# A delta rule with both heads stacked on partitions: 64 columns in place of 128

## The chip, the core and the metric

The kernel runs on one core of a Trainium2 chip. The metric is device time in microseconds (us), the median of several executions. The engines are named as the profile names them: PE is TensorE's matmul, PEld its weight load, DVE is VectorE, ACT is ScalarE, POOL is GpSimd, and SP issues the transfers (DMAs).

## The reference

One inference step of a hybrid layer. 256 prompt tokens and 64 sample tokens (8 sequences of 8) go through RMSNorm and one wide projection. Branch A is an RWKV-7 recurrence with 16 heads of width 64, branch B a gated linear recurrence with 8 heads of 128. Both are projected, gated, merged, projected once more and normalised. The change lies in branch A, whose recurrence per token is

```python
sa = einsum('nhvk,nhk->nhv', s, kk_t)
s = (s * w_t[:, :, None, :] - sa[..., None] * (kk_t * a_t)[:, :, None, :]
     + v_t[..., None] * k_t[:, :, None, :])
y_t = einsum('nhvk,nhk->nhv', s, r_t)
```

A token's state `s` has been changed by every token before it (the delta rule). For a chunk of 64 tokens this is a triangular system: with a strictly triangular matrix `N` of products between keys, the right-hand sides are solved by the inverse of `1 - N`, and the solutions update the state.

## The kernel before

All arithmetic is fp32. Large products are made of three fp32r matmuls (high by high, high by low, low by high): each weight block `raw` of 128 x 1024 is cast by ACT to `whi`, DVE subtracts to `wlo`, and PE multiplies 128 x 128 pieces with `hhi` or `hlo` of 320 token columns, into the PSUM tile `mps`. Call one such matmul a **big** one. Small matmuls of branches A and B are plain fp32; the built program has one matmul for each, and the profile shows two passes of it on PE, each with its own weight load. A transpose is one pass.

The program has three stages. First a start (norm, constants). Then a recorded stage: for each of 8 pairs of heads, eight projection tiles of 48 big matmuls, the function `rwkv` for the pair (two heads of branch A) and `hgrn` (one head of branch B), then seven gate tiles. Last come the projections of the branches (L492 to L494) and the output projection (L1678 to L1684), which the change does not touch.

In the recorded stage nothing is issued when it is written. `V`, `S`, `G`, `T` and `Y` (DVE, ACT, POOL, PE, SP) are proxies that record; `Recorder.order` then deals all operations out by a list schedule: every operation has a cost and a latency from a formula of its shape, dependences are found from the tiles' partitions and columns (in PSUM from partitions alone), big matmuls keep their order, and small matmuls go between them as soon as their operands should be there. So a change of a few shapes moves nearly every row. Every instruction of this stage has the line L199 in the profile (the recorder's call); one goes by its tiles' names. Six PSUM banks are lent to the small products; the profile calls each of them `bank`. The framework that emits the operations in that order adds the semaphore waits itself, and it does so by tile: a matmul that writes a bank waits for a copy that was emitted before it and reads that bank, also where the two touch different partitions.

PE's array can be cut into tiles of rows by columns. Each matmul carries its cut: 128x128 for big and most small ones, 128x32 for `side_by_side` groups of 32-column products, 64x128 and 64x64 for two others. A profile row shows it as the weights' partitions by columns, `128*32`.

Inside `rwkv`, a pair's 256 prompt tokens are four chunks of 64 (`ci`, two outer by two inner), and the names are:

- `g2`: masked products of keys and queries; `nd`: the part to be inverted; `yz`: the inverses of the four chunks, on 128 partitions; `ys`: the samples' inverse; `M`, `pp`, `xt`: pieces with which `yz` is finished.
- `pr`, `psr`: PSUM tiles with the products that the right-hand sides start from, head 0 on partitions 0 to 63, head 1 on 64 to 127. They are the first 28 matmuls of a group of 70, all in 128x32 cuts, whose other 42 are branch B's. `rhs`, `rhs2`: right-hand sides; `uv`: solutions and values; `st`: the state after a chunk, `sf` the same decayed; `bk`, `arp`: keys, and decayed keys and queries.
- `chunks()`: for each chunk, PE multiplies `arp` with `st` (chunks 1 to 3), DVE adds into `rhs`, PE multiplies `yz` with `rhs`, ACT copies into `uv`, PE multiplies `bk` with `uv`, DVE makes `st`, ACT makes `sf`. At the end the state is transposed (`pso`), copied to `so` and stored. `samples()` does it once with `ys`.

Before, the inverse `yz` of one chunk has 64 token rows of one position in the pair of chunks, for both heads side by side in the columns; `rhs` therefore has the two heads side by side too, 128 columns wide, and `st` is a 128 x 128 tile of which the two diagonal blocks are the heads' states:

```python
pu = aps("pu")
T.matmul(pu[:, :128], yz[:, c_, cp]..., rt..., start=True, stop=True)
...
sn = at("st", (128, 128), bufs=4)
V.scalar_tensor_tensor(sn, pd[:, :128], fc, sf, op0=ALU.mult, op1=ALU.add)
```

Of the kernel before, what the change touches and what calls it, by code (L numbers as in the profile page):

```python
# [13 lines left out]
ALU = mybir.AluOpType  # L14
# [5 lines left out]
NT = NP_ + NS  # L20
# [407 lines left out]
def hybrid_step(ctx, tc, x_prompt, x_sample, state_rwkv, state_hgrn, state_shift, norm_g, w_in,  # L428
# [80 lines left out]
    with tc.tile_pool(name="start", bufs=1) as st, \  # L509
# [78 lines left out]
        G.tensor_copy(seqm[HS[1]], seqm[low_])  # L588
        own8 = ctile([128, 8], "own8")
# [242 lines left out]
    def ring(pool, tag, shape, bufs, dt, size, clear=False):  # L832
# [17 lines left out]
        if len(shape) == 2:  # L850
# [5 lines left out]
             "w1": 384, "w2": 320, "w3": 320, "ks": 128, "ye": 192, "ket": 256, "o": NT}  # L856
# [55 lines left out]
    def rwkv(p, r, k, v, za):  # L912
# [129 lines left out]
        for c_ in range(2):  # L1042
            S.copy(nd[HS[c_]], g2[HS[c_], c_:4:2, 0])
# [55 lines left out]
        V.tensor_mul(ys[0:64].rearrange("p h (b j) -> p h b j", j=8), yes[:, :, None, :].to_broadcast([64, 2, 8, 8]),  # L1099
                     seqm[0:64, None, :, None].to_broadcast([64, 2, 8, 8]))  # L1100
        yt = at("yt", (128, 4, 32), tag="uK")
        V.transpose(yt.rearrange("p x (j g) -> p x g j", g=8), ye)
        for q_ in (1, 3, 0, 2):
            (S.copy if q_ % 2 else G.tensor_copy)(yz[quads[q_], q_ // 2, :, :, halves[q_ % 2]],
                                                  yt[quads[q_]].rearrange("p (a h) t -> p a h t", h=2))
# [3 lines left out]
        for cp in range(2):  # L1109
            T.matmul(ps[:, 128 * cp:128 * cp + 128], M[:, cp].rearrange("p h t -> p (h t)"), yz[:, :, cp, :, 32:64], start=True, stop=True)  # L1110
# [7 lines left out]
        for c_ in range(2):  # L1118
            own = quads[2 * c_]
            S.copy(yz[own, c_, :, :, 32:64], ps[own, :256].rearrange("p (a c h t) -> p a c h t", a=2, c=2, h=2)[:, :, c_])  # L1120
# [31 lines left out]
        def chunks():  # L1152
            st_ = None
            for ci in range(4):
                cp, c_ = ci // 2, ci % 2
                tk = HS[c_]
                rt = at("rhs", (128, 2, 64))
                if st_ is None:
                    S.copy(rt[tk, 0], pr[HS[0], 0:64])
                    S.copy(rt[tk, 1], pr[HS[1], 0:64])  # L1160
                    rv = at("rv", (128, 3, 64), tag="ye")
                    S.copy(rv.rearrange("p c v -> p (c v)"), pr[:, 64:256])
                else:
# [12 lines left out]
                sn = at("st", (128, 128), bufs=4)  # L1176
                fc = f[:, 4 + ci:5 + ci]
                if st_ is None:
                    V.tensor_scalar(sn, pd[:, :128], fc, 0.0, op0=ALU.mult, op1=ALU.add)
                else:  # L1180
                    V.scalar_tensor_tensor(sn, pd[:, :128], fc, sf, op0=ALU.mult, op1=ALU.add)
# [15 lines left out]
        def samples():  # L1197
            rhs = at("rhs2", (128, 2, 64))
            S.copy(rhs[0:64, 0], psr[HS[0], :64])
            S.copy(rhs[0:64, 1], psr[HS[1], :64])  # L1200
            yield
            pu = aps("pu2")
            T.matmul(pu[:, :128], ys.rearrange("p h t -> p (h t)"), rhs.rearrange("p h t -> p (h t)"), start=True, stop=True)
            S.copy(uv[0:64, 4, 0], pu[HS[0], 0:64])
# [602 lines left out]
```

## Time and profile before

| | us |
|---|---|
| median of 3 runs | 1070.43 |
| lowest, highest | 1070.11, 1072.08 |
| the profiled execution's own time | 1070.57 |
| its span, first to last instruction | 1068.6 |
| recorded stage, about | 27 to 652 of the span |
| projections of the branches | about 652 to 910 |
| output projection and end | about 910 to the end |

The granted clock was 0.998 of full speed over the span. In rows of groups, the number after the bar is the busy time in us, then the mean of one in ns, then the idle time of the engine before them and what ended it. In rows of the timeline come start, length in us, engine, line, operation, tiles, the weights' cut, shape and count. PE's matmuls are pipelined: a big one is shown 0.31 us long, while the next starts 0.147 us after it, so what one costs is read from starts.

### The profile page before, as it was taken

The page shows a single profiled execution, that of the slowest core. Times are in us where ns is not written, and L with a number is a line of the kernel's source. Part 1 is how long each engine was busy: PE and PEld are TensorE (multiplying, and loading weights), DVE is VectorE, ACT ScalarE, POOL GpSimd, SP SyncE. Part 2 cuts the span into 40 slices and gives each one's busy share as a digit, 9 for nine tenths or more (in the row PEclk, how much of TensorE's full clock was granted, in tenths as well). Part 3 has the DMA queues.
Part 4 walks back from the last instruction along what each step waited for, and adds up shares of the span by engine and source line. Part 5 has one row for each costly group of instructions (what it writes and reads, how often), then busy time and mean ns, then how long its engine had stood idle before and what let it go on. Part 6 is the DMA issues. An engine that isn't in the chain of part 4 may idle for free.

```text
span 1068.6 us, 22991 instructions
## 1 busy us (share of the span) xinstructions
PE 1047.8 (98%) x8740; PEld 1011.1 (95%) x8740; DVE 758.5 (71%) x1608; ACT 696.9 (65%) x1616; POOL 124.1 (12%) x358
## 2 busy tenths in 40 slices
PE   7999999999999999999999999999999999999996
PEld 6999999999999999999999999999999999988886
DVE  8779889988988999989898856544443444446632
ACT  7757888878868878689688698444444444444412
POOL 9511201101111212011112000000000000000000
PEclk9999999999999999999999999999999999999999
DMA  6776585684774864866856837555455554587402
GB/s 203 195 178 180 131 210 139 157 225 122 185 195 120 210 188 119 203 162 158 210 131 178 214 110 206 168 158 164 142 154 150 147 157 143 155 295 245 169 20 98
DMA packets 356369, 178.77 MB, mean 167 GB/s; under 512 B 82013, under 2 KB 345440, under 8 KB 355684
## 3 DMA queue, kind: packets, MB, share of 16 engines
q1 hardware_dynamic: 355892, 176.01, 60.4%
q8 instruction: 68, 1.11, 0.4%
q10 hardware_dynamic: 368, 1.31, 0.3%
q14 instruction: 41, 0.34, 0.1%
HBM read 159.97 MB, written 17.32 MB: 166 GB/s over the span
## 4 chain that ended last, share of the span: by engine, by line
PE 87%; ACT 4%; DVE 4%; DMA 4%; issue 1%; SPq 0%; DVEq 0%; ACTq 0%
PE mps L199 39%; PE bank L199 10%; PE mps L494 5%; PE mps L493 5%; PE mps L492 5%; PE po L1678 3%; PE po L1679 3%; PE po L1680 3%; PE ppa L493 2%; PE ppb L494 2%; PE ppa L494 2%; PE ppb L493 2%; PE ppb L492 2%; PE ppa L492 2%; PE po L1684 1%; PE po L1683 1%
## 5 line engine op out<-in xcount | busy, mean ns | idle before, releaser
L199 PE MATMUL mps<-hhi,whi 128*128 128x320 f32 x1136 | 356.3, 314 | 0.0
L199 PE MATMUL mps<-hhi,wlo 128*128 128x320 f32 x1136 | 355.3, 313 | 0.4 <-DVE wlo L199 0.4
L199 PE MATMUL mps<-hlo,whi 128*128 128x320 f32 x1136 | 355.5, 313 | 0.0
L199 PEld LDWEIGHTS mps<-hhi,wlo 128*128 128x128 f32 x1136 | 213.6, 188 | 2.6 <-issue 1.5
L199 PEld LDWEIGHTS mps<-hlo,whi 128*128 128x128 f32 x1136 | 213.6, 188 | 2.4 <-issue 1.2
L199 PEld LDWEIGHTS mps<-hhi,whi 128*128 128x128 f32 x1136 | 213.7, 188 | 0.9 <-issue 0.4
L199 DVE TENSOR_TENSOR wlo<-raw,whi 128x1024 fp32r<-128x1024 f32 x140 | 171.5, 1225 | 24.9 <-ACT whi L199 23.6
L482 ACT CAST whi<-raw 128x1024 fp32r<-128x1024 f32 x82 | 85.7, 1048 | 146.5 <-PE mps L493 90.4
L483 DVE TENSOR_TENSOR wlo<-raw,whi 128x1024 fp32r<-128x1024 f32 x82 | 100.3, 1225 | 111.6 <-ACT whi L482 111.5
L199 ACT CAST whi<-raw 128x1024 fp32r<-128x1024 f32 x140 | 145.9, 1043 | 47.3 <-DMA raw<-in_w_in_dram 22.4
L494 PE MATMUL mps<-hhi,wlo 128*128 128x320 f32 x400 | 123.7, 309 | 0.1
L493 PE MATMUL mps<-hlo,whi 128*128 128x320 f32 x400 | 123.6, 309 | 0.0
L492 PE MATMUL mps<-hhi,whi 128*128 128x320 f32 x400 | 123.6, 309 | 0.0
L494 PEld LDWEIGHTS mps<-hhi,wlo 128*128 128x128 f32 x400 | 75.1, 188 | 0.3 <-DVE wlo L483 0.3
L492 PEld LDWEIGHTS mps<-hhi,whi 128*128 128x128 f32 x400 | 75.1, 188 | 0.0
L493 PEld LDWEIGHTS mps<-hlo,whi 128*128 128x128 f32 x400 | 75.1, 188 | 0.0
L1667 DVE TENSOR_TENSOR wlo<-raw,whi 128x1024 fp32r<-128x1024 f32 x32 | 38.5, 1222 | 37.5 <-ACT whi L1666 33.0
L1666 ACT CAST whi<-raw 128x1024 fp32r<-128x1024 f32 x32 | 33.0, 1051 | 47.7 <-DMA raw<-in_w_out_dram 19.5
L1678 PE MATMUL po<-whi,mhi 128*128 128x512 f32 x128 | 50.0, 391 | 0.0
L1679 PE MATMUL po<-whi,mlo 128*128 128x512 f32 x128 | 50.0, 391 | 0.0
L1680 PE MATMUL po<-wlo,mhi 128*128 128x512 f32 x128 | 50.0, 391 | 0.0
L492 PE MATMUL ppa<-yah,whi 128*128 128x320 f32 x128 | 39.7, 310 | 1.0 <-ACT yah L1613 1.0
(413 smaller groups left out, 1986.8 us busy)
## 6 DMA issues: line engine op xcount, KB each, us to landing
raw<-in_w_in_dram SPq DMA_DIRECT2D x194, 512.0 KB
raw<-in_w_out_dram SPq DMA_DIRECT2D x32, 512.0 KB
raw<-in_proj_a_dram SPq DMA_DIRECT2D x16, 512.0 KB
raw<-in_proj_b_dram SPq DMA_DIRECT2D x16, 512.0 KB
s<-in_state_hgrn_dram SPq DMA_DIRECT2D x8, 512.0 KB
ww<-scr SPq DMA_DIRECT2D x8, 512.0 KB
out_dram<-s SPq DMA_DIRECT2D x8, 512.0 KB
scrt<-ww SPq DMA_DIRECT2D x32, 120.0 KB
```

The costliest lines, as they stand in the source:

```text
L199: o.fn(*(real(x) for x in o.args), **{k: real(x) for k, x in o.kw.items()})
L482: S.copy(hi[:, ks], raw[:, ks])
L483: sub.tensor_sub(lo[:, ks], raw[:, ks], hi[:, ks].bitcast(F32))
L492: T.matmul(dst, hi[:, q, :], xhi[:, k, :], start=(k == 0), stop=False)
L493: T.matmul(dst, hi[:, q, :], xlo[:, k, :], start=False, stop=False)
L494: T.matmul(dst, lo[:, q, :], xhi[:, k, :], start=False, stop=(k == nk - 1))
L1666: S.copy(hi, raw)
L1667: V.tensor_sub(lo, raw, hi.bitcast(F32))
L1678: T.matmul(pt, h, hi, start=first, stop=False)
L1679: T.matmul(pt, l, hi, start=False, stop=False)
L1680: T.matmul(pt, h, lo, start=False, stop=end)
L1683: T.matmul(pt, h, hi, start=first, stop=False)
```

## The change

In the inverse, head and chunk change places: `yz` is now indexed by pair of chunks, chunk and head, and its 128 partitions hold head by token. The heads are stacked on partitions, block diagonal in the inverse, and everything that was two heads wide becomes 64 columns: `rhs` and `rhs2` (128 x 64), the results of `pr` and `pu` in `chunks()` and `samples()`, the state `st` and `sf`. Right-hand sides are copied or added by one instruction on 128 partitions, not two on 64. The state is made by two DVE instructions of 64 x 64. `nd` is copied by four ACT instructions, not two. The last state's transpose has 64 columns of weights and writes 64 partitions, and one copy takes it out. `ys` is filled on 128 partitions with a mask `seqh` that POOL makes at the start. As many matmuls and transfers are recorded as before.

```diff
+        seqh = ctile([128, 16], "seqh")
+        G.memset(seqh, 0.0)
+        for h in range(2):
+            G.tensor_copy(seqh[HS[h], 8 * h:8 * h + 8], seqm[HS[h]])
...
         for c_ in range(2):
-            S.copy(nd[HS[c_]], g2[HS[c_], c_:4:2, 0])
+            for h in range(2):
+                S.copy(nd[HS[h], :, c_], g2[HS[c_], c_:4:2, 0, h])
...
-        yes = at("yes", (64, 2, 8), tag="dns")
-        Y.dma_start(yes, sample_[1].rearrange("(h p) j -> p h j", h=2))
+        yes = at("yes", (128, 8), tag="dns")
+        Y.dma_start(yes, sample_[1])
...
             for ci in range(4):
-                rt = at("rhs", (128, 2, 64))
+                rt = at("rhs", (128, 64))
                 if st_ is None:
-                    S.copy(rt[tk, 0], pr[HS[0], 0:64])
-                    S.copy(rt[tk, 1], pr[HS[1], 0:64])
+                    S.copy(rt, pr[:, 0:64])
...
-                    T.matmul(ps[:, :128], arp[:, ci, 0].rearrange("p h t -> p (h t)"), st_, start=True, stop=True)
-                    for h in range(2):
-                        V.tensor_add(rt[tk, h], ps[HS[h], 64 * h:64 * h + 64], rv[HS[h], ci - 1])
+                    T.matmul(ps[:, :64], arp[:, ci, 0].rearrange("p h t -> p (h t)"), st_, start=True, stop=True)
+                    V.tensor_add(rt, ps[:, :64], rv[:, ci - 1])
                 yield
                 pu = aps("pu")
-                T.matmul(pu[:, :128], yz[:, c_, cp].rearrange("p h t -> p (h t)"), rt.rearrange("p h t -> p (h t)"), start=True, stop=True)
-                S.copy(uv[tk, ci, 0], pu[HS[0], 0:64])
-                S.copy(uv[tk, ci, 1], pu[HS[1], 64:128])
+                T.matmul(pu[:, :64], yz[:, cp, c_].rearrange("p h t -> p (h t)"), rt, start=True, stop=True)
+                for h in range(2):
+                    S.copy(uv[tk, ci, h], pu[HS[h], 0:64])
...
-                sn = at("st", (128, 128), bufs=4)
...
+                sn = at("st", (128, 64), bufs=4)
+                for h in range(2):
+                    own, new, fc = sn[HS[h]], pd[HS[h], 64 * h:64 * h + 64], f[HS[h], 4 + ci:5 + ci]
...
-                    sf = at("sf", (128, 128))
+                    sf = at("sf", (128, 64))
...
-            T.transpose(ps[:, :128], st_, ident)
+            T.transpose(ps[0:64, :128], st_, ident)
             so = at("so", (64, 2, 64))
-            for h in range(2):
-                S.copy(so[:, h], ps[HS[h], 64 * h:64 * h + 64])
+            S.copy(so.rearrange("p h k -> p (h k)"), ps[0:64, :128])
...
         def samples():
-            rhs = at("rhs2", (128, 2, 64))
-            S.copy(rhs[0:64, 0], psr[HS[0], :64])
-            S.copy(rhs[0:64, 1], psr[HS[1], :64])
+            rhs = at("rhs2", (128, 64))
+            S.copy(rhs, psr[:, :64])
```

Three places in the dealt order. In its rows, a result's shape is partitions by columns, and `waits` names the engines whose semaphores the instruction waits for.

**PE, the group of 70 of the first pair**, from its first row to the first of branch B (`s0t,az` and the first `uv,g` rows make `psr`, the other `uv,g` rows make `pr`). Before:

```order
L199 MATMUL bank_468<-s0t_516,az_519 32x64 x8
L199 MATMUL bank_468<-uv_514,g_0_521 32x64 x4
L199 MATMUL bank_467<-uv_514,g_0_521 32x64 x4
L199 MATMUL bank_467<-uv_514,g_0_521 32x64 [waits DMAHW3_49]
L199 MATMUL bank_467<-uv_514,g_0_521 32x64 x10
L199 MATMUL bank_467<-uv_514,g_0_521 32x64 [waits Activation_49]
L199 MATMUL bank_464<-s_0_528,qz 32x128 x8
```

And in the changed kernel:

```order
L199 MATMUL bank_471<-s0t_520,az_523 32x64 x8
L199 MATMUL bank_471<-uv_518,g_0_525 32x64 [waits DMAHW2_49]
L199 MATMUL bank_471<-uv_518,g_0_525 32x64 x3
L199 MATMUL bank_470<-uv_518,g_0_525 32x64 x4
L199 MATMUL bank_470<-uv_518,g_0_525 32x64 [waits DMAHW3_49]
L199 MATMUL bank_470<-uv_518,g_0_525 32x64 x11
L199 MATMUL bank_472<-s_0_532,qz 32x128 x8
```

The wait of the last `uv,g` matmul for an ACT copy is gone. Such a wait stood four times in the order before, in the groups of pairs 1, 4 (twice) and 8; in the changed order no group of 70 has one behind a copy into `rhs` or `rhs2`.

**ACT, the copies out of `psr` and `pr`** of the same pair. Before:

```order
L199 ACTIVATE dl_557<-F_533 128x1 [waits DVE_49]
L199 COPY rhs_0_544<-bank_468 64x64 [waits PE_49]
L199 COPY rhs_543<-bank_467 64x64 [waits PE_49] x2
L199 COPY ye_524<-bank_467 128x192
L199 COPY rhs_0_544<-bank_468 64x64
L199 ACTIVATE w_0_535<-R_534 128x128 [waits PE_49]
```

And in the changed kernel:

```order
L199 COPY pad_493<-mps 128x8x8 [waits Activation_49]
L199 COPY rhs_0_548<-bank_471 128x64 [waits PE_49]
L199 COPY rhs_547<-bank_470 128x64 [waits PE_49]
L199 COPY ye_528<-bank_470 128x192
L199 ACTIVATE w_0_539<-R_538 128x128 [waits DVE_49,PE_49]
```

Two copies on 128 partitions stand where four on 64 stood; each now reads both heads.

**PE, the transpose of the last state** (`ident,st`), second pair. Before:

```order
L199 MATMUL bank_467<-rl_558,jr_all 128x320 [waits DVE_49]
L199 MATMUL bank_463<-ident,s_0_505 128x128 [waits DMAHW1_49]
L199 MATMUL bank_463<-ident,s_0_505 128x128 x3
L199 MATMUL bank_464<-ident,st_550 128x128 [waits DVE_49]
L199 MATMUL mps<-hlo,whi 128x320
L199 MATMUL mps<-hhi,wlo 128x320
```

And in the changed kernel:

```order
L199 MATMUL mps<-hhi,wlo 128x320
L199 MATMUL mps<-hhi,whi 128x320
L199 MATMUL bank_470<-ident,st_554 64x128 [waits DVE_49]
L199 MATMUL mps<-hlo,whi 128x320
L199 MATMUL mps<-hhi,wlo 128x320
```

It writes 64 partitions where it wrote 128, and its cut in the built program is 128x64, with 128x128 matmuls on both sides; all eight pairs have it so. The other cuts change as often as before.

More of the change, by code (lines that the diff above doesn't have):

```diff
@@ L1094, in rwkv @@
                             prompt_[1].rearrange("(a h c b r) m -> a h b r c m", a=2, h=2, c=2, b=2)[a_, h, 0])
-        yes = at("yes", (64, 2, 8), tag="dns")
-        Y.dma_start(yes, sample_[1].rearrange("(h p) j -> p h j", h=2))
+        yes = at("yes", (128, 8), tag="dns")
+        Y.dma_start(yes, sample_[1])
         ys = at("ys", (128, 2, 64))
-        V.tensor_mul(ys[0:64].rearrange("p h (b j) -> p h b j", j=8), yes[:, :, None, :].to_broadcast([64, 2, 8, 8]),
-                     seqm[0:64, None, :, None].to_broadcast([64, 2, 8, 8]))
+        V.tensor_mul(ys.rearrange("p h (b j) -> p (h b) j", j=8), yes[:, None, :].to_broadcast([128, 16, 8]),
+                     seqh[:, :, None].to_broadcast([128, 16, 8]))
         yt = at("yt", (128, 4, 32), tag="uK")
@@ L1103, in rwkv @@
         for q_ in (1, 3, 0, 2):
-            (S.copy if q_ % 2 else G.tensor_copy)(yz[quads[q_], q_ // 2, :, :, halves[q_ % 2]],
-                                                  yt[quads[q_]].rearrange("p (a h) t -> p a h t", h=2))
+            (S.copy if q_ % 2 else G.tensor_copy)(yz[quads[q_], :, :, q_ // 2, halves[q_ % 2]],
+                                                  yt[quads[q_]].rearrange("p (a c) t -> p a c t", c=2))
         ps = aps("pP")
         for cp in range(2):
-            T.matmul(ps[:, 128 * cp:128 * cp + 128], M[:, cp].rearrange("p h t -> p (h t)"), yz[:, :, cp, :, 32:64], start=True, stop=True)
+            T.matmul(ps[:, 128 * cp:128 * cp + 128], M[:, cp].rearrange("p c t -> p (c t)"),
+                     yz[:, cp].rearrange("p c h t -> p h c t")[:, :, :, 32:64], start=True, stop=True)
         pp = at("pp", (128, 4, 64))
@@ L1119, in rwkv @@
             own = quads[2 * c_]
-            S.copy(yz[own, c_, :, :, 32:64], ps[own, :256].rearrange("p (a c h t) -> p a c h t", a=2, c=2, h=2)[:, :, c_])
+            S.copy(yz[own, :, :, c_, 32:64], ps[own, :256].rearrange("p (a h c t) -> p a h c t", a=2, c=2, h=2)[:, :, c_])
         bp = parts(bon)
@@ L1175, in chunks @@
                 T.matmul(pd[:, :128], bk[:, ci], uv[:, ci].rearrange("p h v -> p (h v)"), start=True, stop=True)
-                sn = at("st", (128, 128), bufs=4)
[L1177 to L1181, printed above, removed]
+                sn = at("st", (128, 64), bufs=4)
+                for h in range(2):
+                    own, new, fc = sn[HS[h]], pd[HS[h], 64 * h:64 * h + 64], f[HS[h], 4 + ci:5 + ci]
+                    if st_ is None:
+                        V.tensor_scalar(own, new, fc, 0.0, op0=ALU.mult, op1=ALU.add)
+                    else:
+                        V.scalar_tensor_tensor(own, new, fc, sf[HS[h]], op0=ALU.mult, op1=ALU.add)
                 st_ = sn
@@ L1197, in samples @@
         def samples():
-            rhs = at("rhs2", (128, 2, 64))
-            S.copy(rhs[0:64, 0], psr[HS[0], :64])
-            S.copy(rhs[0:64, 1], psr[HS[1], :64])
+            rhs = at("rhs2", (128, 64))
+            S.copy(rhs, psr[:, :64])
             yield
             pu = aps("pu2")
-            T.matmul(pu[:, :128], ys.rearrange("p h t -> p (h t)"), rhs.rearrange("p h t -> p (h t)"), start=True, stop=True)
-            S.copy(uv[0:64, 4, 0], pu[HS[0], 0:64])
-            S.copy(uv[0:64, 4, 1], pu[HS[1], 64:128])
+            T.matmul(pu[:, :64], ys.rearrange("p h t -> p (h t)"), rhs, start=True, stop=True)
+            for h in range(2):
+                S.copy(uv[0:64, 4, h], pu[HS[h], 0:64])
             fh = at("fh", (128, 8), dt=F32R)
@@ L1253, in rwkv @@
                 for h, o_, w in parts4:
-                    work.append(((py[o_:o_ + 32, cols_], states[ci - 1][:, o_:o_ + 32], arp[:, ci, 1, h]),
+                    work.append(((py[o_:o_ + 32, cols_], states[ci - 1][:, 32 * w:32 * w + 32], arp[:, ci, 1, h]),
                                  dict(start=True, stop=False)))
```

2 lines of the change are left out of this document (1 added, 1 removed).

## Prediction

> **What bounds the kernel now.** I read the page's first part first, then the busy times by stage, then PE's waits. The page:
>
> ```profile
> span 1068.6 us, 22991 instructions
> PE 1047.8 (98%) x8740; PEld 1011.1 (95%) x8740; DVE 758.5 (71%) x1608; ACT 696.9 (65%) x1616; POOL 124.1 (12%) x358
> ```
>
> The busy times of the stretch that holds the recorded stage (time, busy time of PE, PEld, DVE, ACT, POOL, clock, DMA share):
>
> ```profile
> 27.00:652.00 625.00, 620.33 (x6097) 606.40 (x6096) 539.83 (x1311) 499.13 (x1313) 99.64 (x305) 1.00 0.67 171
> ```
>
> PE is busy for 620.33 of 625 us, DVE for 540, ACT for 499. So PE sets the end of this stage: only what shortens PE's own stream, or takes away one of its few waits, is worth time. A busy PE is not PE at its peak, so each price below is read from starts. The two waits that matter here, in the list of who waited for whom (total us, times, longest):
>
> ```profile
> PE bank L199 <- DMA s<-in_state_rwkv_dram: 1.9, 3, 0.8
> PE bank L199 <- ACT rhs L199: 1.7, 4, 0.8
> ```
>
> The second has the name of a tile that the change rewrites. The sum is made against the profiled execution's 1070.57 us, 0.14 above the median of 1070.43.
>
> **Part 1: 64 matmuls with half the columns.** Per pair, four products with `yz`, one with `ys` and three of `arp` with `st` go from 128 to 64 moving columns: 64 matmuls of two passes each in the program. The trace of before has a neighbour of just that shape, `att,vt` with 64 columns, and 0.5 us after it a 128-column one, `uv,bk`:
>
> ```profile
> 123.71 0.31 PE L199 MATMUL mps<-hhi,wlo 128*128 128x320 f32 x1
> 123.86 0.33 PE L199 MATMUL bank<-att,vt 128*128 128x64 f32 x2
> 124.00 0.39 PE L199 MATMUL mps<-hhi,whi 128*128 128x320 f32 x1
> 124.23 0.30 PE L199 MATMUL mps<-hlo,whi 128*128 128x320 f32 x1
> 124.37 0.31 PE L199 MATMUL mps<-hhi,wlo 128*128 128x320 f32 x1
> 124.52 0.38 PE L199 MATMUL bank<-uv,bk 128*128 128x128 f32 x2
> 124.66 0.39 PE L199 MATMUL mps<-hhi,whi 128*128 128x320 f32 x1
> 124.89 0.31 PE L199 MATMUL mps<-hlo,whi 128*128 128x320 f32 x1
> ```
>
> From the big matmul before the small one to the second big one after it: 124.23 − 123.71 = 0.52 us with 64 columns, 124.89 − 124.37 = 0.52 us with 128. Two big ones alone take 2 × 0.147 = 0.29, so either small matmul costs PE 0.23 us. The columns are not what is paid; both have 128 x 128 weights, and the two weight loads are the same. Term: 0 (bounds: 0, and −7.4 us if the price went with the columns, 64 × 0.115).
>
> Here a page of the Trainium skill pulls two ways. "TensorE: Matmul & The Clock Gate", section "Back-to-back issue gap", has an isolated gap of N/2.4 + 2.5 ns; by it, as an estimate, each of 128 passes would be 27 ns shorter and the sum 3.4 us lower. Its section "LDWEIGHTS (loading the stationary operand)" has a load paid by weight columns alone, 107 ns for 128, which would hide that. The trace's two 0.52 us agree with the second.
>
> **Part 2: a wait inside the group of 70 goes.** The group of the second pair is clean (first two rows below, from `s0t,az` to the next big matmul); those of pairs 1, 4 and 8 are not:
>
> ```profile
> 181.27 0.43 PE L199 MATMUL bank<-s0t,az 128*32 128x64 f32 x16
> ...
> 183.29 0.41 PE L199 MATMUL mps<-hlo,whi 128*128 128x320 f32 x1
> 108.55 0.43 PE L199 MATMUL bank<-s0t,az 128*32 128x64 f32 x16
> ...
> 109.85 0.24 PE L199 MATMUL bank<-uv,g 128*32 128x64 f32 x1 [0.32 <-ACT rhs L199]
> ...
> 111.15 0.41 PE L199 MATMUL mps<-hhi,whi 128*128 128x320 f32 x1
> 327.31 0.43 PE L199 MATMUL bank<-s0t,az 128*32 128x64 f32 x16
> ...
> 328.14 0.75 PE L199 MATMUL bank<-uv,g 128*32 128x64 f32 x34 [0.30 <-ACT rhs L199]
> ...
> 329.18 0.24 PE L199 MATMUL bank<-uv,g 128*32 128x64 f32 x1 [0.29 <-ACT rhs L199]
> ...
> 330.46 0.41 PE L199 MATMUL mps<-hlo,whi 128*128 128x320 f32 x1
> 612.05 0.43 PE L199 MATMUL bank<-s0t,az 128*32 128x64 f32 x16
> ...
> 613.80 0.30 PE L199 MATMUL bank<-uv,g 128*32 128x64 f32 x2 [0.77 <-ACT rhs L199]
> ...
> 615.13 0.41 PE L199 MATMUL mps<-hhi,wlo 128*128 128x320 f32 x1
> ```
>
> The clean group takes 2.02 us, the others 2.60, 3.15 and 3.08: 0.58 + 1.13 + 1.06 = 2.8 us more. The rows in between name the cause, and the order shown above has the wait: ACT's copy of head 0 out of `psr` or `pr` is emitted as soon as head 0's products are there, and head 1's last matmul, which writes the same bank, then waits for it. The 0.3 us and 0.77 us in the brackets are less than the loss, because they count from the modelled end of the earlier matmul. In the changed kernel the copy reads both heads, so it comes behind all matmuls of its tile, and none waits for it. Behind the waiting matmul stands the rest of the group and every big matmul, so all of it is PE's time. Term: −2.8 us; at the other end 0, if other ACT copies turn up in the groups.
>
> **Part 3: eight transposes get a cut of their own.** The last state's transpose was one pass in a 128x128 cut and is one in 128x64 now, alone among big matmuls. Before, and a group with another cut (64x128, also 128 moving columns):
>
> ```profile
> 139.89 0.31 PE L199 MATMUL mps<-hhi,wlo 128*128 128x320 f32 x1
> 140.04 0.27 PE L199 MATMUL bank<-ident,st 128*128 128x128 f32 x1
> 140.06 0.39 PE L199 MATMUL mps<-hhi,whi 128*128 128x320 f32 x1
> 140.29 0.31 PE L199 MATMUL mps<-hlo,whi 128*128 128x320 f32 x1
> ...
> 132.20 0.31 PE L199 MATMUL mps<-hhi,whi 128*128 128x320 f32 x1
> 132.44 1.39 PE L199 MATMUL bank<-arp,bk 64*128 64x128 f32 x20
> 133.75 0.42 PE L199 MATMUL mps<-hlo,whi 128*128 128x320 f32 x1
> 134.01 0.39 PE L199 MATMUL bank<-vm,k 128*128 128x512 f32 x1
> L199 PE MATMUL bank<-arp,bk 64*128 64x128 f32 x160 | 11.1, 282 | 0.0
> ```
>
> The old transpose costs 140.29 − 139.89 − 0.29 = 0.11 us. Into the other cut it is 0.24 us from start to start (not 0.147). The last of the 20 passes starts at 132.44 + 1.39 − 0.28 = 133.55, 0.20 before the next big matmul, and the one after that comes 0.26 later. A single pass between two such borders costs 0.24 + 0.20 + 0.26 − 0.29 = 0.41 us, 0.30 more than before: 8 × 0.30 = +2.4 us. No row has a 128x64 cut. Low end: it leaves as the old transpose does (0.02 in place of 0.20), +0.12 each, +1.0 us. High end: it needs two passes, as every other fp32 matmul here, 0.11 us more each, +3.3 us. I take 2.4, from the row with as many columns.
>
> A rule of the Trainium skill speaks against this part: "TensorEngine Tiling (Array Packing)", section "Restrictions and Gotchas", lists transpose mode with fp32 input among what column tiling excludes, which would be the two passes of the high end. The trace has no such row, and I stay with one pass.
>
> **Part 4: what DVE, ACT, POOL and SP do.** The nearest rows, by tile:
>
> ```profile
> L199 DVE SCALAR_TENSOR_TENSOR st<-bank,f,sf x24: 340/350/353, 118.6 to 636.0; 128x128 f32<-128x128 f32 x24
> L199 DVE TENSOR_TENSOR rhs<-bank,ye x48: 208/222/228, 115.9 to 632.8; 64x64 f32<-64x64 f32 x48
> L199 ACT COPY rhs<-bank x32: 190/208/212, 109.2 to 616.1; 64x64 f32<-64x64 f32 x32
> L199 ACT COPY rhs<-uv x32: 281/296/300, 113.7 to 635.8; 32x128 f32<-32x128 f32 x32
> L199 ACT COPY big<-g x16: 391/405/408, 60.7 to 573.6; 64x256 f32<-64x256 f32 x16
> ```
>
> DVE: 32 states of 0.35 become 64 halves, at 0.222 each as an estimate (+3.0 us); 48 additions of 0.222 become 24 (−5.3). ACT: 16 copies of `nd` at 0.405 become 32 of about 0.296 (+3.0), 32 copies into `rhs` become 16 (−3.3), 16 of the last state become 8 (about −1). DVE has 2.3 us less and ACT 1.3, spread over 625 us in which PE's big matmuls cover both; without that cover it would be some 0.4 us per pair, off the chain of the chunks. POOL's three instructions more fall into the start, where PE's own transposes cover them. Transfers are as many as before. Term: 0.
>
> **The sum.** 0 − 2.8 + 2.4 + 0 = −0.4 us: 1070.2 for a profiled execution, **1070.0 us** in the median. The terms' bounds make −1.8 to +3.3 around it without part 1's far end. To that comes the dealing: nearly every row has moved, and PE's other waits of this stage are dealt anew. Where each lands I can't read from the order; the 1.9 us of the first wait above is a measure of what such a redeal can give or take.
>
> **The rivals.**
>
> *The redeal pays.* The wait for the transfer of the next state (1.9 us, 3 times) goes as well. For it: the order of SP now issues the store of the old state earlier than before in most pairs, and its reload with it. Against: the transpose that waits for it has moved ahead too. With the forecast's −0.4: −2.3, 1068.1 us, and lower where part 3 comes at its low end (1066.7).
>
> *Columns are paid after all.* Part 1 at −7.4 us: 1062.6 us. Against it stands the 0.52 us twice.
>
> *A new wait takes the old one's place; slower.* The second group of each pair, 48 products in 128x32 cuts, needs `uv` of the last chunk, which ACT copies. In the changed order the matmuls of the last chunk wait for these copies in the middle of the group in five pairs, before in one. If ACT is late there (a cast of a whole weight block may stand ahead), PE stops inside the group as in part 2, for 0.58 to 1.06 us a time: five times 2.9 to 5.3, so 1072.9 to 1075.3 us. It decides from five such stops, 2.6 us. Against: the scheduler holds the whole group back until the copies should be done, and the one pair that had this wait before lost nothing by it.
>
> *The change does not do it.* The groups of 70 keep stops behind other copies out of the same banks: part 2 is 0 and the time is 1070.4 + 2.4 = 1072.8. The order shows no such wait behind `rhs`, so this is the least likely but one.
>
> **How the numbers follow.** Forecast (all terms as taken, redeal within ±1.5 us): 0.60, 1068.2 to 1071.8. The redeal pays: 0.19. Columns: 0.04. New wait: 0.12. Not done: 0.05. A measurement of this kernel can tell about 0.2%, 2.1 us, from no change. Faster by more than that: the columns and most of the redeal, some of the forecast's edge, 0.23. Slower: most of the last two, 0.14. Same: 0.63. The range leaves out the columns, the new wait's upper part and a little at either edge: 1066.6 to 1073.2 us.
>
> **What would show it.** In the profile after: `rhs,yz` with 64 columns still 0.23 us between big matmuls (part 1); the groups of 70 all near 2.0 us and no PE wait on ACT `rhs` (part 2); `ident,st` as `128*64`, with 0.24 us into it and 0.2 and 0.26 out (part 3); the stretch from 27 us to the first branch projection as long as before within 2 us. I am wrong if the narrow matmuls are cheaper, if the transposes cost several tenths more than 0.41, or if PE shows a new wait of more than 2 us in all.

## The result, and the profile after

The changed kernel takes **1066.0 us** (median of five runs, 1064.74 to 1067.38); the kernel before 1071.49 (five runs, 1070.11 to 1073.57). The ratio is 0.9948, with a 95% interval of 0.9935 to 0.9961. So the changed kernel is 5.5 us faster, where the prediction had 0.4 us and "no change": the time lies 0.6 us under the predicted range, and clear of noise. (1.06 of the 5.5 us is the kernel before's own median, which two more runs raised from 1070.43 us, the base of the forecast, to 1071.49.) The profiled execution after took 1065.99 us, its span is 1063.8 us and the granted clock 0.997.

Where the time went is read from the starts at the stages' borders: the last big matmul of the recorded stage, the first and the last matmul of the output projection. Rows of the timeline, first of before, then of after:

```profile
652.01 0.31 PE L199 MATMUL mps<-hhi,wlo 128*128 128x320 f32 x1
943.06 0.39 PE L1678 MATMUL po<-whi,mhi 128*128 128x512 f32 x1
1060.00 0.28 PE L1684 MATMUL po<-wlo,ms 128*128 128x256 f32 x1
```

```profile
647.80 0.31 PE L199 MATMUL mps<-hhi,wlo 128*128 128x320 f32 x1
937.81 0.39 PE L1681 MATMUL po<-whi,mhi 128*128 128x512 f32 x1
1054.75 0.28 PE L1687 MATMUL po<-wlo,ms 128*128 128x256 f32 x1
```

The recorded stage ends 4.21 us earlier. The branch projections take 290.01 us in place of 291.05, 1.04 less, although the change does not touch them: at their beginning before has 1.0 us of wait for ACT's `yah`, and after has none of it. The output projection takes 116.94 us in both; it starts at 943 us, not near 910 as the table ahead of the prediction has it. The row of the wait for `yah`, in before's list of who waited for whom:

```profile
PE ppa L492 <- ACT yah L1613: 1.0, 1, 1.0
```

The busy times of the stretch from 27 to 652 us in the changed kernel (same columns as before; 4 us of it are already the next stage):

```profile
27.00:652.00 625.00, 622.74 (x6126) 609.90 (x6125) 547.62 (x1321) 503.33 (x1312) 103.57 (x305) 1.00 0.67 173
```

PE still sets the end. The list of who waited for whom of the changed kernel, the rows of the recorded stage (total us, times, longest):

```profile
PE bank L199 <- POOL fd L199: 1.5, 3, 0.6
PE bank L199 <- DVE wst L199: 0.4, 1, 0.4
PE bank L199 <- issue: 0.4, 1, 0.4
```

Both rows shown of before, the waits for `rhs` and for the load of `s`, are gone. A wait for POOL's `fd` is new.

Such a list counts idle time from the modelled end of the matmul ahead, and a busy PE hides part of a stall. So I made a second account, from starts alone: in the recorded stage of every profiled execution below, each step from one PE start to the next is compared with the usual step of its kind (the lowest fifth over all 14 profiles, by the two tiles, by whether a small matmul stands ahead and by the place in a group). Steps over 0.1 us longer than usual are called **stalls**, all else **work** (the expectations below give it without the steps that are longer by less than 0.1 us; these are about 20 us in every kernel, so they say 594 where the table has 616, and the first of them count stalls in an earlier, narrower way, in which before has 5.2 us):

| | stalls, us | of them `uv,g` in the groups of 70 | work, us |
|---|---|---|---|
| before | 10.0 | 2.5 | 615.5 |
| after | 5.6 | 0 | 615.7 |

The work is the same; the 4.2 us of this stage are stalls (4.4 less, and 0.2 more work). Before has 2.5 us for the copies into `rhs`, 2.5 at the transposes of `s` (late loads), 0.7 inside `ks,s`, 0.5 at `es`. After has 2.0 at `fd` and 0.6 at a product of `rh`.

The three parts of the prediction, in rows of the changed kernel: a narrow `rhs,yz` alone among big matmuls, the group of 70 of the second pair (its ends), and the last state's transpose.

```profile
109.56 0.31 PE L199 MATMUL mps<-hhi,whi 128*128 128x320 f32 x1
109.71 0.33 PE L199 MATMUL bank<-rhs,yz 128*128 128x64 f32 x2
109.85 0.39 PE L199 MATMUL mps<-hlo,whi 128*128 128x320 f32 x1
110.08 0.30 PE L199 MATMUL mps<-hhi,wlo 128*128 128x320 f32 x1
...
134.22 0.31 PE L199 MATMUL mps<-hhi,wlo 128*128 128x320 f32 x1
134.37 0.27 PE L199 MATMUL bank<-ident,st 128*64 128x128 f32 x1
134.39 0.39 PE L199 MATMUL mps<-hhi,whi 128*128 128x320 f32 x1
134.62 0.31 PE L199 MATMUL mps<-hlo,whi 128*128 128x320 f32 x1
...
173.34 0.43 PE L199 MATMUL bank<-s0t,az 128*32 128x64 f32 x16
173.59 0.74 PE L199 MATMUL bank<-uv,g 128*32 128x64 f32 x40
...
175.37 0.41 PE L199 MATMUL mps<-hhi,whi 128*128 128x320 f32 x1
```

`rhs,yz` with 64 columns: 110.08 − 109.56 = 0.52 us, as with 128. The group: 2.03 us, and its 40 `uv,g` passes stand in one row without a bracket; in all eight pairs it takes 1.89 to 1.92 us from its first to its last start. The transpose, now `128*64`: 134.62 − 134.22 = 0.40 us, the same as before's 140.29 − 139.89, so it costs 0.11 us and no border; the other seven cost the same within 0.01 us.

### The profile page after: what moved, and what is told of

Read it like the earlier page. It is cut to its first block, busy times and chain, and to the rows that moved or that the text cites. A ratio compares the mean times of both kernels' runs of the same rounds, so it can differ in the third digit from the quotient of the medians.

```text
span 1063.8 us, 23012 instructions
## 1 busy us (share of the span) xinstructions
PE 1045.8 (98%) x8740; PEld 1010.4 (95%) x8740; DVE 763.5 (72%) x1616; ACT 697.9 (66%) x1608; POOL 127.8 (12%) x361
## 4 chain that ended last, share of the span: by engine, by line
PE 94%; POOL 2%; ACT 1%; DVE 1%; DMA 1%; issue 0%; DVEq 0%; ACTq 0%; POOLq 0%
PE mps L199 47%; PE bank L199 10%; PE mps L494 5%; PE mps L493 5%; PE mps L492 5%; PE po L1682 3%; PE po L1681 3%; PE po L1683 3%; PE ppb L493 2%; PE ppb L494 2%; PE ppb L492 2%; PE ppa L494 2%; PE ppa L493 2%; PE ppa L492 2%; PE po L1687 1%; PE po L1686 1%
## 5 line engine op out<-in xcount | busy, mean ns | idle before, releaser
L199 PE MATMUL mps<-hhi,whi 128*128 128x320 f32 x1136 | 356.7, 314 | 0.0
L199 PE MATMUL mps<-hlo,whi 128*128 128x320 f32 x1136 | 355.7, 313 | 0.0
L199 PE MATMUL mps<-hhi,wlo 128*128 128x320 f32 x1136 | 354.7, 312 | 0.0
L199 PEld LDWEIGHTS mps<-hhi,whi 128*128 128x128 f32 x1136 | 213.6, 188 | 3.2 <-issue 2.3
L199 PEld LDWEIGHTS mps<-hlo,whi 128*128 128x128 f32 x1136 | 213.7, 188 | 1.2 <-issue 0.4
L199 PEld LDWEIGHTS mps<-hhi,wlo 128*128 128x128 f32 x1136 | 213.6, 188 | 1.1 <-issue 0.4
L199 DVE TENSOR_TENSOR wlo<-raw,whi 128x1024 fp32r<-128x1024 f32 x140 | 171.4, 1224 | 23.2 <-ACT whi L199 21.7
L199 ACT CAST whi<-raw 128x1024 fp32r<-128x1024 f32 x140 | 146.2, 1044 | 44.0 <-PE mps L199 34.1
L493 PE MATMUL ppb<-ybl,whi 128*128 128x320 f32 x128 | 39.7, 310 | 0.4 <-DVE ybl L1617 0.4
```

What stands on the lines that cost most here:

```text
L199: o.fn(*(real(x) for x in o.args), **{k: real(x) for k, x in o.kw.items()})
L493: T.matmul(dst, hi[:, q, :], xlo[:, k, :], start=False, stop=False)
```

## The experiments

The theory after the result, **L**: the changed operations are worth the stalls behind `rhs`, some 2.5 us, and the rest of the 5.5 us came from the new deal, which set other stalls. Against it stood **N**, that narrow tiles gain by themselves, and **G**, that the changed operations make the whole gain in any order. All runs in one table; the ratio is to the kernel before on the same chip in the same series. Stalls and work are of the one profiled execution of each.

| kernel | ratio to before (95%) | stalls, us | behind `rhs` | work, us |
|---|---|---|---|---|
| after | 0.9948 (0.9935 to 0.9961) | 5.6 | 0 | 615.7 |
| b_whole | 1.0007 (0.9998 to 1.0016) | 8.9 | 0 | 616.0 |
| a_split | 1.0000 (0.9992 to 1.0009) | 12.0 | 1.1 | 615.9 |
| b_spare21 | 0.9960 (0.9948 to 0.9973) | 7.1 | 2.0 | 616.5 |
| a_spare21 | 0.9948 (0.9935 to 0.9962) | 5.3 | 0 | 616.0 |
| b_spare19 | 0.9958 (0.9943 to 0.9972) | 8.0 | 2.1 | 615.9 |
| a_spare19 | 1.0019 (1.0005 to 1.0033) | 11.8 | 0 | 615.9 |
| a_mm64 | 0.9934 (0.9920 to 0.9948) | 5.3 | 0 | 615.9 |
| a_lead | 0.9929 (0.9916 to 0.9943) | 6.7 | 0 | 616.4 |
| a_deal_b | 0.9985 (0.9976 to 0.9995) | 9.6 | 0 | 615.1 |
| b_deal_a | 0.9959 (0.9944 to 0.9974) | 6.8 | 0 | 615.8 |
| b_deal_a_w | 1.0020 (1.0009 to 1.0031) | 12.8 | 8.0 | 616.9 |
| a_own_fd | 0.9926 (0.9910 to 0.9943) | 3.0 | 0 | 615.7 |

Before itself has 10.0, 2.5 and 615.5. A name that begins with `b` has the tiles of before, one with `a` those of the changed kernel. The work lies within 615.1 to 616.9 us in all fourteen, and the time follows the stalls by and large (a profile is one execution, the ratio is made of many; the clearest exception, a_spare19, stands below).

### The wait taken away, the wait put back

**b_whole**: the kernel before, in which the planner believes that the copies of head 0 read all partitions, so it places them behind the whole tile.

```diff
-                o.uses.append((f"loan{n}", *span_of(self.moved(x, off))[1:], j == 0, True))
+                p0, p1, m = span_of(self.moved(x, off))[1:]
+                o.uses.append((f"loan{n}", *((0, 128) if self.whole else (p0, p1)), m, j == 0, True))
...
+                    book.whole = True
                     S.copy(rt[tk, 0], pr[HS[0], 0:64])
                     S.copy(rt[tk, 1], pr[HS[1], 0:64])
+                    book.whole = False
```

> The kernel before, in which the planner takes the first chunk's and the samples' copies into the right-hand sides as readers of all 128 partitions of their PSUM tile; same instructions, same widths, only the order is dealt anew. Theory W (the wait inside the group of 70 is the change's own gain): all eight groups take 1.87 to 1.92 us from first to last start, no row of uv,g waits for ACT, and the time is 2.5 us under before, plus or minus 1.9 for the new deal: 0.996 to 1.000 of before, middle 0.9976. Rival N (narrow tiles are the gain, 64 matmuls with half the columns): the time is that of before within the deal, 1.000 plus or minus 0.0018.

Measured: 1072.61 us, 1.0007 of before. No wait for `rhs` is left, and seven of the groups of 70 take 1.87 to 1.90 us, the eighth 3.64 for another stall (1.75 us inside `ket`). Other stalls came in their place: 1.0 us at `yz,uE`, 0.5 at `fd`, and outside this stage one of 1.4 us in the output projection. So the wait went and the time did not. The number is rival N's (1.000) and just misses theory W's range, but stalls as large as the wait came in their place, so by itself this run settles nothing; it showed that one new deal can cost what the wait gave.

**a_split**: the changed kernel with the copies per head again.

```diff
-                    S.copy(rt, pr[:, 0:64])
+                    for h in range(2):
+                        S.copy(rt[HS[h]], pr[HS[h], 0:64])
...
-            S.copy(rhs, psr[:, :64])
+            for h in range(2):
+                S.copy(rhs[HS[h]], psr[HS[h], :64])
```

> The changed kernel with the copies into the right-hand sides of the first chunk and of the samples made per head again, two instructions for one; everything stays 64 columns wide. Theory W: three of the eight groups of 70 hold a wait for ACT again, each such wait costs 0.5 to 1.0 us, so 1.5 to 3 us more than the changed kernel, about 0.997 of before, plus or minus 1.9 us for the deal. Rival N: as the changed kernel, 0.995 of before, and the groups take 1.90 us.

Measured: 1072.18 us, the time of before. Two groups, not three, hold the wait (0.53 us each, 1.1 together), in line with the price, but by the ratios 5.6 us came in all: this deal also has 2.9 us at late loads of `s` and 1.4 in a group of 70 right behind `ks,s`. The expectation was missed on the high side, and N is not saved by it: all tiles were 64 wide here.

### Controls: a new deal and nothing else

Four runs changed one planning constant by 1 ns, in the kernel before and in the changed one; the work to be dealt is the same.

```diff
-    AHEAD, SLIP, SOON, SPARE = 300, 0, 1500, 20
+    AHEAD, SLIP, SOON, SPARE = 300, 0, 1500, 21
```

> Control: the kernel before, with the planner's allowance for each ACT, DVE and POOL operation at 21 ns in place of 20. The work is the same, about 1500 rows of PE's order differ. Theory D (a new deal alone is worth up to 2 us either way): the time lies within 0.998 to 1.002 of before, but with other stalls on PE's stream than those of before (other places and causes, sum 3 to 7 us of irregular waits in the recorded stage, before has 5.2). Rival (the deal does not matter): within 0.0005 of before.

> Control: the changed kernel with the same allowance of 21 ns. Theory D: 0.993 to 0.998 of before, that is within 2 us of the changed kernel's 0.9948, with other stalls on PE's stream (the three waits for POOL's fd, 2.0 us together in the changed kernel, can go or move). Rival (the change's 5.5 us are all its own work): 0.9948 within 0.0005.

> Second control of the kernel before: allowance 19 ns. Its order holds four waits of a uv,g matmul for ACT's copies in the groups of 70 (before: four; first control: four). Theory D: regular work 593.5 to 594.5 us, irregular waits 5 to 12 us, time 0.996 to 1.002 of before. Theory G: 0.999 to 1.001 of before, the first control's 0.996 having been the exception.

> Second control of the changed kernel: the planner's allowance at 19 ns in place of 20. Theory D (deal luck of some us in each kernel, regular work equal): regular PE work of the recorded stage 594 to 595 us as in all kernels so far, irregular waits 4 to 12 us, time 0.993 to 1.000 of before. Theory G (the change itself makes the gain, whatever the deal): 0.993 to 0.996 of before as the changed kernel and its first control.

Measured: the kernel before came to 0.9960 and 0.9958, over 4 us faster, with the waits behind `rhs` still there. The changed kernel came to 0.9948, as it was (which the rival of that control expected too), and to 1.0019. Not all of this last figure is the deal: ten of a_spare19's eleven executions have a granted clock of 0.990 to 0.996, where the kernel before had 0.996 to 0.998 in the same series; the one at 0.998, which is the profiled one, took 1072.33 us, 0.9983 of before. Why the clock was lower there is open. Theory G expected 0.993 to 0.996 of every deal of the changed kernel, and falls with either figure. Theory D's bounds were too narrow as well: 0.9960 lies outside its first, 0.9958 and 1.0019 just outside those of the second pair. What it said of the work held within about 1 us, and the stalls came to 5.3 to 11.8 us, in other places each time. What made the last one slow, besides the clock, stands in its list of waits, the rows of the recorded stage:

```profile
PE bank L199 <- DMA s<-in_state_rwkv_dram: 3.3, 1, 3.3
PE bank L199 <- DVE es L199: 1.9, 2, 1.0
PE bank L199 <- issue: 1.2, 1, 1.2
```

One late load of `s` costs 3.3 us. The same rows in the first control of before:

```profile
PE bank L199 <- ACT rhs L199: 1.2, 4, 0.3
PE bank L199 <- ACT yz L199: 1.0, 1, 1.0
PE bank L199 <- DVE rl L199: 0.8, 1, 0.8
PE bank L199 <- DMA s<-in_state_rwkv_dram: 0.7, 1, 0.7
```

Four waits for `rhs`, as in before, but the load of `s` takes 0.7 us where before lost 1.9. So comparing two deals of two kernels can't price the change: its own part is smaller than what the deal moves.

### The order held still

For the next three runs the list schedule was replaced. Both kernels record 8227 operations, and all but a few have a counterpart in the other. So one kernel's order, and its choice of the lent banks, can be given to the other's operations; a copy made of two takes the place of the later one.

```diff
     def order(self):
         self.link()
+        rank = [int.from_bytes(raw_[2 * j:2 * j + 2], "little") for j in range(len(raw_) // 2)]
+        self.home = {n: int(c) for n, c in enumerate(HOME)}
...
+        heap = [(rank[o.n], o.n) for o in self.ops if not o.npred]
+        while heap:
+            _, n = heapq.heappop(heap)
...
+            done.append(o)
```

**a_deal_b**: the changed kernel's operations in the order of before.

> The changed kernel with the dealt order of the kernel before: every operation is emitted at the place its counterpart has there (a merged copy at the place of the later of the two), with the same lent banks. So the tiles change and the order does not. Theory L (the change is worth the waits in the group of 70 alone, and the rest of the 5.5 us was the new deal): 2.5 us under before, 0.9977, plus or minus 0.0007; all groups of 70 at 1.87 to 1.92 us, the waits of the transposes of s for their load still there. Theory G (the changed operations themselves make 5.5 us): 0.9948.

**b_deal_a**: the operations of before in the changed kernel's order.

> The reverse: the kernel before, all its tiles 128 columns wide, with the dealt order of the changed kernel; its two copies into the right-hand sides stand together where the changed kernel's one copy stands, behind the group. Theory L: no wait for ACT in the groups of 70, and the time of the changed kernel, 0.9948 of before, plus or minus 0.0010. Theory G: 0.9975 to 1.000.

**b_deal_a_w**: as b_deal_a, with one thing moved, head 0's copies into the middle of seven groups.

> As the run of the kernel before in the changed kernel's order, but with the copy of head 0 into rhs and rhs2 emitted right behind head 0's last product, so that in seven of the eight groups of 70 head 1's last matmuls wait for ACT twice. Theory L with the price of a pair of such waits as before showed it (3.15 us against 2.02 for a group with two): 7 times 1.1, 7.7 us over that run, 1.002 of before. Rival (such waits are made up for later, by slack that other waits had): less than 3 us over that run.

In these kernels, and in a_own_fd below, the recorder's call is line L405, not L199.

Measured, all in one series: a_deal_b 1070.68 us, 0.9985 of before (0.9976 to 0.9995), b_deal_a 1067.18, 0.9959 (0.9944 to 0.9974). Theory L's 0.9977 and 0.9948 lie inside the intervals (the medians miss the ranges it gave by 0.0001 each), G's 0.9948 for the first and 0.9975 or more for the second lie outside (the second just). So in the order of before the changed operations are worth 1.7 us (0.5 to 2.6 by the interval), of 2.5 that L expected. And the tiles of before, 128 columns wide and without the wait, run in the changed kernel's order at about its time, 0.9959 against 0.9948 from another series; in the two traces PE's rows of this stage come in the same order, tile for tile. With that N falls: the gain is there without a narrow tile.

What became of the rest of the 2.5 us in a_deal_b: no stall behind `rhs` is left, but its stalls are 9.6 us, only 0.4 under before, since the others rose from 7.5 us. One group of 70, the seventh pair's, still takes 2.84 us, against the expectation (2.54 in before, also not for `rhs`), and the list of waits has:

```profile
PE bank L405 <- DMA s<-in_state_rwkv_dram: 2.7, 3, 1.0
```

Three waits for the load of `s`, as in before, but 2.7 us, not 1.9. The first of them, in before and in a_deal_b:

```profile
291.74 0.31 PE L199 MATMUL mps<-hhi,wlo 128*128 128x320 f32 x1
292.70 0.66 PE L199 MATMUL bank<-ident,s 128*128 128x128 f32 x4 [0.65 <-DMA s<-in_state_rwkv_dram]
...
291.91 0.31 PE L405 MATMUL mps<-hhi,wlo 128*128 128x320 f32 x1
293.23 0.65 PE L405 MATMUL bank<-ident,s 128*128 128x128 f32 x4 [1.01 <-DMA s<-in_state_rwkv_dram]
```

PE does not come earlier here; the load does come later. SP issues it at 286.85 us, 286.46 in before. Why the load is later with the order held is open, and so is whether the missing 0.8 us are these.

b_deal_a_w against b_deal_a is the cleanest price of the wait: 1074.81 − 1067.18 = 7.6 us for seven groups, expected 7.7. Its row in the list of waits:

```profile
PE bank L405 <- ACT rhs L405: 5.5, 14, 0.6
```

And one of its groups, in the timeline:

```profile
173.79 0.43 PE L405 MATMUL bank<-s0t,az 128*32 128x64 f32 x16
174.04 0.28 PE L405 MATMUL bank<-uv,g 128*32 128x64 f32 x4
174.89 0.65 PE L405 MATMUL bank<-uv,g 128*32 128x64 f32 x32 [0.57 <-ACT rhs L405]
175.87 0.25 PE L405 MATMUL bank<-uv,g 128*32 128x64 f32 x2 [0.33 <-ACT rhs L405]
...
177.19 0.41 PE L405 MATMUL mps<-hhi,whi 128*128 128x320 f32 x1
```

Fourteen waits, 5.5 us by the list and 8.0 by starts, 7.6 us of time. This group takes 177.19 − 173.79 = 3.40 us, against 2.03 above. The rival, that such waits are made up for later (less than 3 us), falls for this order. In a_deal_b, where the waits were taken away, other stalls did grow by some 2 us.

### What a 128x64 cut costs

**a_mm64**: in the changed kernel, the samples' product cut into one matmul per head, a plain product in the cut that the transposes have.

```diff
-            T.matmul(pu[:, :64], ys.rearrange("p h t -> p (h t)"), rhs, start=True, stop=True)
+            for h in range(2):
+                T.matmul(pu[HS[h], :64], ys[:, h], rhs, start=True, stop=True)
```

> The changed kernel with the samples' product of ys and rhs2 cut in two, one matmul per head with 64 columns of weights (cut 128x64) writing its own 64 partitions: 8 matmuls more, no transposes touched. Read by starts, from the big matmul before the product to the second big one after it, where the product stands alone among big ones: 0.52 us with one matmul of two passes. Theory X (the prediction's price: a cut of its own is paid in and out, and only a transpose was spared it): 0.52 plus two more passes of 0.055 to 0.11 each plus 0.30, 0.9 to 1.05 us. Theory Y (64 weight columns on 128 rows are no change of the array): 0.6 to 0.75 us. The time as a whole moves by the deal as well, 0.993 to 1.000 of before under either.

The one place of the sixth pair, alone among big matmuls:

```profile
469.27 0.31 PE L199 MATMUL mps<-hhi,wlo 128*128 128x320 f32 x1
469.42 0.31 PE L199 MATMUL mps<-hhi,whi 128*128 128x320 f32 x1
469.65 0.34 PE L199 MATMUL bank<-rhs,ys 128*64 128x64 f32 x4
469.92 0.42 PE L199 MATMUL mps<-hlo,whi 128*128 128x320 f32 x1
470.18 0.27 PE L199 MATMUL bank<-ident,es 128*128 128x128 f32 x1
```

From the big matmul ahead to the start after the next big one: 470.18 − 469.42 = 0.76 us, between the two expectations (0.6 to 0.75 and 0.9 to 1.05) and far nearer theory Y's. The single starts decide against Y all the same. The borders are there: 0.23 to 0.24 us into the group, not 0.147, and 0.26 from the first big matmul after it to the next start, as at the 64x128 group that the prediction quoted. The sum is less than theory X had, because the passes are cheaper: the two heads' passes start 6 to 7 ns apart, side by side. So a plain product pays for a 128x64 cut and a transpose does not.

### The waits for POOL

One of the new waits of the changed kernel, in its timeline; of the rows of all engines those of DVE, POOL and PE's `fd` product:

```profile
348.81 1.23 DVE L199 TENSOR_TENSOR wlo<-raw,whi 128x1024 fp32r<-128x1024 f32 x1
...
348.85 1.66 POOL L199 TENSOR_TENSOR fd<-id,fq 128x256 fp32r<-128x256 f32 x1 [6.84 <-PE bank L199]
...
349.95 0.90 DVE L199 TENSOR_TENSOR bk<-bk 128x320 f32<-128x320 f32 x1
...
350.56 0.38 PE L199 MATMUL bank<-fd,jr_sum 128*128 128x256 f32 x1 [0.43 <-POOL fd L199]
```

And by tile, with minimum, median and maximum in ns:

```profile
L199 POOL TENSOR_TENSOR fd<-id,fq x16: 614/618/1662, 50.4 to 577.3; 128x256 fp32r<-128x256 f32 x16
```

POOL's product takes 0.62 us in the median, and 1.66 when it starts 0.04 us behind DVE's wide subtraction. Before had the same stretching (0.62 median, 1.50 at most), but PE had no need of those results yet.

**a_lead** gives the two products of `fd` more room and deals all anew:

```diff
-                T.matmul(pf[:, 256 * hf:256 * hf + 256], jr_sum, fd.rearrange("p s k -> p (s k)"), start=True, stop=True)
+                T.matmul(pf[:, 256 * hf:256 * hf + 256], jr_sum, fd.rearrange("p s k -> p (s k)"), start=True, stop=True).margin = 1600
```

> The changed kernel with one number of the planner changed: the two matmuls of fd are dealt 1600 ns after POOL's product is planned to end, not 400. In the changed kernel POOL's product took 0.62 us, but 1.3 to 1.66 us in five of 16 cases, and PE waited in three of them, 2.0 us by starts. Theory P (those waits come from POOL's longer time and add to the end): no wait of PE for fd over 0.1 us, and the time 2 us under the changed kernel, 0.993 of before, plus or minus 1.9 us for what the new deal does elsewhere. Rival (waits only change place): 0.995 of before, with the sum of irregular waits as in the changed kernel, 5.8 us.

Measured: 0.9929. No wait for `fd` is left, but stalls are 6.7 us: 1.2 at `es`, 1.0 at `rl`, more at `wlo`. So theory P's time came, but not in its way: the waits for POOL went, and others came, which is again the deal.

**a_own_fd** keeps the changed kernel's own order, replayed as above, and moves only these products, the first of a pair by 8 big matmuls, the second by 16. No operation changes; in the list of ranks that is given to the replay, 16 of 8227 entries are set anew (`i`: the number of big matmuls ahead of the product):

```diff
+    i = bisect.bisect(br, rank[m])
+    rank[m] = br[i + 8 * (1 + q_ % 2) - 1] + 0.5
```

> The changed kernel with its own dealt order, in which only the two matmuls of fd per pair are moved, the first behind the 8th big matmul after its place, the second behind the 16th (1.2 and 2.4 us). Nothing else is dealt anew. Theory P: the three waits for POOL (2.0 us by starts) go and nothing comes in their place, 2 us under the changed kernel, 0.993 of before, plus or minus 0.0007. Rival: the waits that follow in the stage (for loads, for DVE) take the time up, 0.995.

Measured: 1064.52 us, 0.9926 of before (0.9910 to 0.9943), the fastest here. Expected were 2 us under the changed kernel; by the ratios it is 2.4 us. The two were timed in different series and their intervals overlap, so I rest the gain on the trace: stalls fall from 5.6 to 3.0 us with the same work, the list has no wait for POOL, and the stage's last big matmul starts at 645.26 us, where the changed kernel had 647.80. In the trace PE's other 6082 rows of the stage keep their order. The row in the timeline:

```profile
645.26 0.31 PE L405 MATMUL mps<-hhi,wlo 128*128 128x320 f32 x1
```

And `fd` by tile:

```profile
L405 POOL TENSOR_TENSOR fd<-id,fq x16: 616/668/1663, 49.7 to 575.9; 128x256 fp32r<-128x256 f32 x16
```

POOL's product still takes 1.56 to 1.66 us in three of the 16 cases (1.30 to 1.66 in five of the changed kernel's); PE only no longer stands behind it.

## Why the prediction was wrong

**What bounds the kernel: right.** PE's stream set the end, and the time followed its stalls by and large.

**Part 1, the columns: right.** 0.52 us from big to second big with 64 columns as with 128; the work of the stage is 615.5 us before and 615.7 after. The two passes come 0.055 us apart, where 128 columns had 0.11, but the next big matmul then starts 0.085 us behind the second pass, where it had 0.03. The rival "columns are paid after all" falls.

**Part 2, the wait in the group of 70: right, mechanism and price.** It went in all eight groups. Taken as 2.8 us from whole groups, 2.5 by single starts. In the order of before its removal, with the rest of the change, brought 1.7 us, and put back in seven groups in a fixed order it cost 7.6.

**Part 3, the transposes: wrong, and the step of the forecast that failed.** The prediction gave a transpose in a 128x64 cut the borders of the 64x128 group, +2.4 us in all, at least +1.0. Measured: 0.11 us each, as before, so 0 us, which its bounds (+1.0 to +3.3) left out. Its reading of the cut held for a plain product of that cut (0.23 to 0.24 us in, 0.26 out) and not for a transpose; the row it was taken from has products. The rule named against this part, from the Trainium skill, "TensorEngine Tiling (Array Packing)", section "Restrictions and Gotchas", that column tiling and the transpose mode of fp32 exclude each other, fits the row in another way than I read it: the transpose ran without a border and in one pass, as if in the full array. That it did is argued from the starts, not shown. With 0 in place of 2.4 the sum is −2.8 us, 1067.6, which lies inside the predicted range; the measured 1066.0 needs the next step as well.

**Part 4, the other engines: right as a term, wrong in size.** By tile, in the changed kernel, DVE's halves of the state take 0.284 us, not 0.222 (64 × 0.284 − 32 × 0.35 = +7.0 us, not +3.0), so DVE has some 1.7 us more, not 2.3 less:

```profile
L199 DVE SCALAR_TENSOR_TENSOR st<-bank,f,sf x48: 268/284/292, 111.7 to 628.2; 64x64 f32<-64x64 f32 x48
```

No run shows a cost of it: the tiles of before in the same order gave the time of the changed kernel within the intervals.

**The redeal: the second step that failed, named but put at 0 with too little room.** The prediction allowed 1.5 us either way in the forecast and 1.9 for "the redeal pays". In the result it gave about 2.7 us: 5.5 less the 2.8 of part 2, or more by the fixed orders (5.5 − 1.7 = 3.8). The trace adds up to the same: stalls other than those behind `rhs` fell from 7.5 to 5.6 us, the work rose by 0.2, and the branch projections were 1.04 us shorter. Against the forecast's own base, before's first median, the error is 1070.0 − 1066.0 = 4.0 us, 2.4 of part 3 and 1.6 of the redeal. The mechanism of that rival was right, the wait for the load of `s` went; with it went other stalls. The controls show the size to allow: changing nothing but one constant by 1 ns, before moved by −4.3 us and the changed kernel by +7.6 (0.9948 to 1.0019 of 1071), or by +3.7 in the one execution of a_spare19 at full clock (0.9983). By these few draws, a range for a change that deals this stage anew needs some 4 us to either side of the sum; 4 us around 1070.43 − 2.8 would have held it, 1063.6 to 1071.6.

**The other rivals.** The new wait in the group of 48 did not come: none of its steps is a stall in the changed kernel. "The change does not do it" falls with part 2.

What stays open: why this load of `s`, or this subtraction on DVE, comes late in one deal and not in another, and whether the changed kernel is better over many deals. Three deals of each, without the runs that meddle with the waits, give 0.9960, 0.9958 and 1 for before, 0.9948, 0.9948 and 1.0019 (0.9983 at full clock) for the change; that does not tell them apart. The fixed order does, by 1.7 us.

## What to carry to other kernels

Where a scheduler deals the whole program anew, one timing of a change is a draw from two lotteries: look at the granted clock of every execution first, then move a neutral constant by a hair, see how far the time goes, and allow that much in the range; to price the change itself, replay one kernel's order with the other's operations. A copy that reads half of a PSUM tile can stop the matmuls that still write the other half, in the middle of a packed group; here one copy on all partitions was worth more for that than for the instruction it saved. And once stalls are told from work by starts, a wait can be moved out of the way one at a time, as a_own_fd did, without a new deal.

## What the runs showed of the hardware that I had not expected

- A transpose whose weights are `128*64` stands among 128x128 matmuls at no extra cost (0.11 us), while a plain product of the same cut starts 0.23 to 0.24 us after the big matmul ahead (the transpose 0.15), and behind it the second start comes 0.26 us after the first (0.23 behind the transpose).
- Two 64-column halves of one array, each with its own head, start 6 to 7 ns apart (a_mm64), where two passes of a full 128x128 product with as many columns come 55 ns apart.
- POOL's two-operand product went from 0.62 to 1.66 us beside DVE's wide two-operand subtraction of 1.23 us, and DVE's next product took 0.90 us where the same form takes 0.49 elsewhere. The Trainium skill, "SBUF — State Buffer", section "Who interferes with whom", has the two engines share one pair of ports as an exclusive lock; the rows agree with that. What they add is where it shows: as a stall of PE, two steps away.
